# Batched 64x64 matmul: A loaded as row pairs, half-empty block stationaries, one store per group

## The chip, the cores and the metric

The kernel runs on one core of one Trainium2 chip. The metric is the device time of one execution in microseconds (us); smaller is better. A batch is one of 1024 independent products; a group is the 32 batches that one turn of the kernel's loop handles.

## The reference

Inputs `a` and `b` are float32 arrays of 1024 x 64 x 64, drawn from a normal distribution. The output is `np.matmul(a, b)` in float32: 1024 independent products C = A B of 64 x 64 matrices.

```
a = randn(1024, 64, 64); b = randn(1024, 64, 64)
return np.matmul(a, b).astype(np.float32)
```

The arithmetic on the chip is in bfloat16 with float32 sums: the loads convert float32 to bfloat16 on their way into SBUF.

## The kernel before

The loop over 32 groups is written out in full (Python `range`), so every instruction below stands 32 times in the program. Tiles come from pools that rotate: three buffers for the inputs (`a_in`, `b_in`), two for the transposed A in SBUF (`at_sb`), three for the output tile (`c_sb`), two for each of the two PSUM tiles (`at_psum`, `c_psum`). A planner derives all semaphores from which instruction reads and writes which tile; each engine works through its instructions in the order of the program, and POOL issues its DMAs in that order too.

One group does this:

- **Loads (L52, L60), issued from POOL.** Two DMAs bring `a`, two bring `b`, in the order a, b, a, b. Each fills 64 of the 128 partitions: partition = a row of a matrix, then 16 matrices, then the 64 elements of the row. One row of one matrix is contiguous in DRAM, so each DMA moves 1024 pieces of 64 float32, 256 bytes read and 128 bytes (bfloat16) written.
- **Transposes (L71) on TensorE.** A matrix multiply contracts over the partition, so A is needed with k on the partitions. Eight 128x128 transposes (against an identity) turn the 32 matrices of `a_in` into `at_psum`, one PSUM bank.
- **Copy (L77) on DVE.** One copy of 128 x 1024 bfloat16 brings `at_psum` into `at_sb`.
- **Products (L86) on TensorE.** 32 matmuls with a 64 x 64 stationary (A transposed) and a 64-column moving operand (B). Even and odd batches use opposite halves of the partitions and write opposite halves of `c_psum`.
- **Copy (L95) on ACT.** One copy of 128 x 1024 float32 brings `c_psum` (two banks) into `c_sb`.
- **Stores (L98), issued from SP.** Two DMAs, one for each half of the partitions, with 1024 pieces of 256 bytes each.

Ahead of the loop POOL builds the identity. On TensorE the transposes of a group stand in the program behind the matmuls of the group before.

Of the kernel before, what the change touches and what calls it, by code (L numbers as in the profile page):

```python
# [1 line left out]

# [5 lines left out]


@with_exitstack
def kernel(
    ctx: ExitStack,
    tc: tile.TileContext,
    a: bass.AP,
    b: bass.AP,
    out: bass.AP,
):
    nc = tc.nc

    B, M, K = a.shape
    _, _, N = b.shape
    assert (M, K, N) == (64, 64, 64)

    GROUP = 32
    HALF = GROUP // 2
    NT = HALF // 2
    dt_in = mybir.dt.bfloat16
    n_groups = B // GROUP

    BATCH_ELEMS = M * K

    consts = ctx.enter_context(tc.tile_pool(name="consts", bufs=1))
    ab_pool = ctx.enter_context(tc.tile_pool(name="ab", bufs=3))
    at_pool = ctx.enter_context(tc.tile_pool(name="at", bufs=2))
    c_pool = ctx.enter_context(tc.tile_pool(name="c", bufs=3))
    psum_t = ctx.enter_context(tc.tile_pool(name="psum_t", bufs=2, space=bass.MemoryType.PSUM))
    psum_c = ctx.enter_context(tc.tile_pool(name="psum_c", bufs=2, space=bass.MemoryType.PSUM))

    identity = consts.tile([128, 128], dt_in)  # L40
    make_identity(nc, identity)

    def dram_ap(tensor_ap: bass.AP, offset: int, dims):
        return bass.AP(tensor=tensor_ap.tensor, offset=offset, ap=[list(d) for d in dims])

    for g in range(n_groups):
        base = g * GROUP

        a_in = ab_pool.tile([128, HALF, 64], dt_in, name="a_in")
        b_in = ab_pool.tile([128, HALF, 64], dt_in, name="b_in")  # L50
        for h in (0, 1):
            nc.gpsimd.dma_start(  # L52
                out=a_in[64 * h : 64 * h + 64, :, :],
                in_=dram_ap(
                    a,
                    (base + HALF * h) * BATCH_ELEMS,
                    [[64, 64], [BATCH_ELEMS, HALF], [1, 64]],
                ),
            )
            nc.gpsimd.dma_start(  # L60
                out=b_in[64 * h : 64 * h + 64, :, :],
                in_=dram_ap(
                    b,
                    (base + h) * BATCH_ELEMS,
                    [[64, 64], [2 * BATCH_ELEMS, HALF], [1, 64]],
                ),
            )

        at_psum = psum_t.tile([128, NT, 128], dt_in, name="at_psum")
        for t in range(NT):  # L70
            nc.tensor.transpose(  # L71
                at_psum[:, t, :],
                a_in[:, 2 * t : 2 * t + 2, :],
                identity,
            )
        at_sb = at_pool.tile([128, NT, 128], dt_in, name="at_sb")
        nc.vector.tensor_copy(out=at_sb, in_=at_psum)  # L77

        c_psum = psum_c.tile([128, 2, 8, 64], mybir.dt.float32, name="c_psum")
        for i in range(GROUP):  # L80
            h = i % 2
            tblk = (i % HALF) // 2
            chalf = i // HALF
            bank = i // 16
            slot = (i // 2) % 8
            nc.tensor.matmul(  # L86
                out=c_psum[64 * h : 64 * h + 64, bank, slot, :],
                lhsT=at_sb[64 * h : 64 * h + 64, tblk, 64 * chalf : 64 * chalf + 64],
                rhs=b_in[64 * h : 64 * h + 64, i // 2, :],
                start=True,  # L90
                stop=True,
            )

        c_sb = c_pool.tile([128, 2, 8, 64], mybir.dt.float32, name="c_sb")
        nc.scalar.copy(out=c_sb, in_=c_psum)  # L95

        for h in (0, 1):
            nc.sync.dma_start(  # L98
                out=dram_ap(
                    out,  # L100
                    (base + h) * BATCH_ELEMS,
                    [[64, 64], [2 * BATCH_ELEMS, 16], [1, 64]],
                ),
                in_=c_sb[64 * h : 64 * h + 64, :, :, :],
            )


# [1 line left out]
_INS = ['a', 'b']  # L109
_OUTS = [((1024, 64, 64), 'float32')]  # L110


# [23 lines left out]
```

## Time and profile before

| what | value |
|---|---|
| device time, median of 4 runs | 222.24 us (221.8 to 222.96) |
| the profiled execution, device time | 222.3 us |
| the profiled execution, span of its instructions | 220.5 us |
| TensorE matmul busy | 31% of the span |
| DVE busy, ACT busy | 10%, 15% |
| POOL busy (issuing loads) | 47% |
| read from HBM, written to HBM | 33.55 MB, 16.78 MB |

The span runs from the first to the last instruction; the device time of the same execution is 1.8 us longer. Busy shares are averages over the whole span. The DMA share of a stretch is the mean number of packets that one of the 16 DMA engines had in hand, so it can exceed 1. The GB/s of the profile count bytes as written, and a load writes half of the bytes that it reads. A packet here is one contiguous piece; each DMA adds 16 packets of 4 bytes that raise its semaphore.

### The profile page before, as it was taken

To read this page: it belongs to the slowest core of one execution; us is meant where nothing else is said; L and a number is where in the kernel's file an instruction comes from. 1 tells how busy PE (TensorE), PEld (TensorE's weight loads), DVE (VectorE), ACT (ScalarE), POOL (GpSimd) and SP (SyncE) were. 2 spreads that over 40 slices of the span, in tenths; PEclk is the share of its full clock that TensorE was granted. 3 is DMA by queue.
4 is the path that set the end of the run, shared out by engine and by line. 5 is a ranking of instruction groups with operands and counts; after the bars stand their busy time and mean duration, and the time that the engine had idled before them with its cause. 6 is when DMAs were issued, how large, how long until landed. Compare 5 with 4: busy or idle time off the path is not lost.

```text
span 220.5 us, 3108 instructions
## 1 busy us (share of the span) xinstructions
PE 68.1 (31%) x1280; PEld 55.1 (25%) x1280; DVE 22.1 (10%) x32; ACT 33.7 (15%) x33; POOL 104.7 (47%) x134
## 2 busy tenths in 40 slices
PE   0462231233441134431234422233422233322340
PEld 0352121123331133321133322133312133311230
DVE  0120011011110111110111110111110111100110
ACT  2111110111101111101111101111011111011110
POOL 8997434365444455444455435454445554441000
DMA  8999999999999999999999999999999999999974
GB/s 53 146 184 157 157 158 158 157 159 156 158 158 157 158 157 159 156 157 157 159 156 157 159 157 158 157 159 157 157 157 159 157 157 158 157 157 159 162 129 95
DMA packets 199695, 33.77 MB, mean 153 GB/s; under 512 B 199680, under 2 KB 199680, under 8 KB 199680
## 3 DMA queue, kind: packets, MB, share of 16 engines
q0 software_dynamic: 133120, 16.79, 117.8%
q1 hardware_dynamic: 66560, 16.78, 55.7%
q8 instruction: 10, 0.16, 0.3%
q14 instruction: 5, 0.04, 0.0%
HBM read 33.55 MB, written 16.78 MB: 228 GB/s over the span
## 4 chain that ended last, share of the span: by engine, by line
DMA 88%; POOL 5%; issue 3%; PE 0%; ACT 0%; POOLq 0%; ACTq 0%
DMA a_in<-in_a_dram 78%; DMA b_in<-in_b_dram 10%; POOL a_in L52 3%; POOL b_in L60 2%; PE c_psum L86 0%; ACT c_sb L95 0%; POOL identity masks.py:199 0%; POOL identity masks.py:197 0%; POOLq masks.py:199 0%; ACTq L95 0%; POOLq L131 0%; POOLq L60 0%; POOLq L120 0%
## 5 line engine op out<-in xcount | busy, mean ns | idle before, releaser
L60 POOL DMA_DIRECT2D b_in<-in_b_dram x64 | 52.9, 827 | 52.3 <-DMA b_in<-in_b_dram 50.7
L52 POOL DMA_DIRECT2D a_in<-in_a_dram x64 | 53.0, 828 | 42.4 <-DMA a_in<-in_a_dram 37.6
L71 PE MATMUL at_psum<-identity,a_in 128*128 128x128 bf16 x256 | 32.4, 306 | 118.0 <-DMA a_in<-in_a_dram 118.0
L95 ACT COPY c_sb<-c_psum 128x1024 f32<-128x1024 f32 x32 | 32.4, 1012 | 180.6 <-PE c_psum L86 180.6
L71 PEld LDWEIGHTS <-a_in 128*128 128x128 bf16 x256 | 24.8, 137 | 121.3 <-issue 121.3
L86 PE MATMUL c_psum<-b_in,at_sb 64*64 64x64 bf16 x1024 | 35.8, 239 | 27.8 <-DVE at_sb L77 25.1
L77 DVE COPY at_sb<-at_psum 128x1024 bf16<-128x1024 bf16 x32 | 22.1, 691 | 190.1 <-PE at_psum L71 190.1
L86 PEld LDWEIGHTS <-at_sb 64*64 64x64 bf16 x1024 | 30.3, 151 | 37.5 <-DVE at_sb L77 33.6
L95 ACT ACT_TABLE_LOAD x1 | 1.3, 1283 | 0.7 <-PEq L120 0.7
masks.py:199 POOL TENSOR_SCALAR_AFFINE_SELECT identity<-identity 128x128 bf16<-128x128 bf16 x1 | 0.3, 306 | 0.1
masks.py:197 POOL MEMSET identity<- 128x128 bf16 x1 | 0.2, 205 | 0.3 <-POOLq L120 0.3
L120 POOL MEMSET const-float32-0.0<- 128x1 f32 x1 | 0.1, 99 | 0.2 <-issue 0.2
L120 POOL MEMSET const-bfloat16-1.0<- 128x1 bf16 x1 | 0.1, 102 | 0.0
L120 POOL MEMSET const-uint8-127<- 128x1 uint8 x1 | 0.1, 102 | 0.0
L120 POOL MEMSET const-float32-1.0<- 128x1 f32 x1 | 0.1, 99 | 0.0
## 6 DMA issues: line engine op xcount, KB each, us to landing
out_dram<-c_sb SPq DMA_DIRECT2D x64, 256.0 KB, 9.7
a_in<-in_a_dram POOLq DMA_DIRECT2D x64, 128.0 KB, 12.8
b_in<-in_b_dram POOLq DMA_DIRECT2D x64, 128.0 KB, 12.9
```

Of the source, the lines that this page charges most:

```text
L52: nc.gpsimd.dma_start(out=a_in[64 * h : 64 * h + 64, :, :], in_=dram_ap(a, (base + HALF * h) * BATCH_ELEMS, [[64, 64], [BATCH_ELEMS, HALF] ...
L60: nc.gpsimd.dma_start(out=b_in[64 * h : 64 * h + 64, :, :], in_=dram_ap(b, (base + h) * BATCH_ELEMS, [[64, 64], [2 * BATCH_ELEMS, HALF], [ ...
L71: nc.tensor.transpose(at_psum[:, t, :], a_in[:, 2 * t : 2 * t + 2, :], identity,)
L77: nc.vector.tensor_copy(out=at_sb, in_=at_psum)
L86: nc.tensor.matmul(out=c_psum[64 * h : 64 * h + 64, bank, slot, :], lhsT=at_sb[64 * h : 64 * h + 64, tblk, 64 * chalf : 64 * chalf + 64], ...
L95: nc.scalar.copy(out=c_sb, in_=c_psum)
L120: nc = _bacc.Bacc("TRN2", target_bir_lowering=False, num_devices=1)
```

## The change

- **Loads of A.** `a_pk` holds two consecutive rows of one matrix on each partition: partition p of block u has the 128 consecutive float32 that start at element 128 p of the four matrices 4u to 4u+3. Four DMAs per group, each for two blocks and all 128 partitions, replace two; each has 256 pieces of 512 bytes read and 256 bytes written. The order on POOL becomes a, a, b, a, a, b. The loads of B stay as they are.
- **Transposes.** Still eight of 128x128. Each now gives even rows of four matrices on partitions 0 to 63 and odd rows on 64 to 127.
- **Copies from PSUM.** One DVE copy becomes four copies of 64 partitions x 512 elements, two on DVE and two on ACT, into two tiles: `se_sb` for the even rows and `so_sb` for the odd rows. For each pair of batches the first one's k stands on partitions 0 to 63 with columns 0 to 31, the second one's on partitions 64 to 127 with columns 32 to 63. The other two quarters hold zeros.
- **Zeros.** The three pairs of these tiles are allocated once, and 12 memsets on DVE ahead of the loop write their zeros.
- **Products.** Still 32 matmuls with 64 columns each way, but each contracts over all 128 partitions: two batches at a time, even rows or odd rows. The output has 32 rows of each batch.
- **Copies of C.** One ACT copy becomes a DVE copy and an ACT copy, one for each bank of `c_ps`. They interleave even and odd rows in `c_sb`, so that each partition holds two consecutive rows.
- **Stores.** One DMA of 128 partitions per group replaces two; it has 1024 pieces of 512 bytes.

Buffer counts stay: three for inputs and output, two for each PSUM tile; the stationary tiles have three where `at_sb` had two.

```diff
-        a_in = ab_pool.tile([128, HALF, 64], dt_in, name="a_in")
+        a_pk = ab_pool.tile([128, NBLK, 128], dt_mm, name="a_pk")
+        AW = 2
         for h in (0, 1):
-            nc.gpsimd.dma_start(
-                out=a_in[64 * h : 64 * h + 64, :, :],
-                in_=dram_ap(
-                    a,
-                    (base + HALF * h) * BATCH_ELEMS,
-                    [[64, 64], [BATCH_ELEMS, HALF], [1, 64]],
-                ),
-            )
+            for u in range(h * NBLK // 2, (h + 1) * NBLK // 2, AW):
+                nc.gpsimd.dma_start(
+                    out=a_pk[:, u : u + AW, :],
+                    in_=dram_ap(
+                        a,
+                        (base + 4 * u) * BE,
+                        [[128, 128], [4 * BE, AW], [1, 128]],
+                    ),
+                )
...
+    for i in range(ST_BUFS):
...
+        nc.vector.memset(se_i[0:64, :, 32:64], 0.0)
+        nc.vector.memset(se_i[64:128, :, 0:32], 0.0)
+        nc.vector.memset(so_i[0:64, :, 32:64], 0.0)
+        nc.vector.memset(so_i[64:128, :, 0:32], 0.0)
...
-        nc.vector.tensor_copy(out=at_sb, in_=at_psum)
+        nc.vector.tensor_copy(out=st_dst(se_sb, 0, 0), in_=at_src(0, 0))
+        nc.scalar.copy(out=st_dst(se_sb, 64, 32), in_=at_src(0, 1))
+        nc.scalar.copy(out=st_dst(so_sb, 0, 0), in_=at_src(64, 0))
+        nc.vector.tensor_copy(out=st_dst(so_sb, 64, 32), in_=at_src(64, 1))
...
+        for s in range(NPAIR):
+            hc = s % 2
+            slot = s // 2
+            for eps, st_tile in ((0, se_sb), (1, so_sb)):
+                nc.tensor.matmul(
+                    out=c_ps[64 * hc : 64 * hc + 64, eps, slot, :],
+                    lhsT=st_tile[:, s, :],
+                    rhs=b_in[:, s, :],
...
-        nc.scalar.copy(out=c_sb, in_=c_psum)
+        nc.vector.tensor_copy(out=c_sb[:, :, 0, :], in_=c_ps[:, 0])
+        nc.scalar.copy(out=c_sb[:, :, 1, :], in_=c_ps[:, 1])
-        for h in (0, 1):
-            nc.sync.dma_start(
...
+        nc.sync.dma_start(
+            out=dram_ap(
+                out,
+                base * BE,
+                [[128, 128], [4 * BE, NPAIR // 2], [1, 128]],
+            ),
+            in_=c_sb,
+        )
```

## Rows read from the trace of the kernel before

**Rows 1.** The page: shares of the span in the chain that ended last.
```profile
DMA 88%; POOL 5%; issue 3%; PE 0%; ACT 0%; POOLq 0%; ACTq 0%
```
**Rows 2.** The page's DMA queues: packets, MB, share of 16 engines' span.
```profile
q0 software_dynamic: 133120, 16.79, 117.8%
q1 hardware_dynamic: 66560, 16.78, 55.7%
```
**Rows 3.** Stretches: busy of PE, PEld, DVE, ACT, POOL; granted clock, DMA share, GB/s.
```profile
11.00:13.00 2.00, 1.22 (x22) 0.95 (x22) 0.69 (x1) 0.00 (x0) 2.00 (x4) 1.00 2.43 155
...
40.00:60.00 20.00, 6.42 (x120) 5.18 (x120) 2.07 (x3) 3.60 (x4) 10.13 (x14) 1.00 1.89 157
100.00:120.00 20.00, 6.43 (x120) 5.18 (x120) 2.08 (x3) 2.96 (x4) 9.55 (x13) 1.00 1.84 157
180.00:200.00 20.00, 6.22 (x120) 5.10 (x120) 2.07 (x3) 2.93 (x4) 9.55 (x12) 1.00 1.80 158
...
216.50:218.50 2.00, 0.00 (x0) 0.00 (x0) 0.00 (x0) 0.00 (x0) 0.00 (x0) 1.00 0.95 203
```
**Rows 4.** DMA queue of code loading in the 1 us from 57.5: packets, MB, share.
```profile
q14 instruction: 1, 0.01, 1.9%
```
**Rows 5.** Chain that ended last, in order of time: start, us, what.
```profile
11.50 0.69 POOL a_in L52
12.19 7.55 DMA b_in<-in_b_dram
...
19.77 0.49 issue
20.26 0.80 POOL b_in L60
21.06 15.68 DMA a_in<-in_a_dram
36.74 0.28 issue
37.03 13.19 DMA a_in<-in_a_dram
```
**Rows 6.** Line L52: durations of its DMA instruction in ns; issue to landing in us.
```profile
L52 POOL DMA_DIRECT2D a_in<-in_a_dram x64: 808/811/990, 1.3 to 197.1; - x64
...
DMA to landing us min/median/max: 3.3/12.8/17.4
```
**Rows 7.** Timeline of one group in the middle: start, us, engine, line, what [idle before].
```profile
104.08 1.01 PE L71 MATMUL at_psum<-identity,a_in 128*128 128x128 bf16 x8 [4.60 <-DMA a_in<-in_a_dram]
...
105.13 0.69 DVE L77 COPY at_sb<-at_psum 128x1024 bf16<-128x1024 bf16 x1 [6.76 <-PE at_psum L71]
105.62 0.81 POOL L60 DMA_DIRECT2D b_in<-in_b_dram  x1 [0.57 <-DMA b_in<-in_b_dram]
105.88 0.93 PEld L86 LDWEIGHTS <-at_sb 64*64 64x64 bf16 x32 [1.05 <-DVE at_sb L77]
105.88 1.06 PE L86 MATMUL c_psum<-b_in,at_sb 64*64 64x64 bf16 x32 [0.78 <-DVE at_sb L77]
...
107.03 1.01 ACT L95 COPY c_sb<-c_psum 128x1024 f32<-128x1024 f32 x1 [6.44 <-PE c_psum L86]
```
**Rows 8.** Timeline of the opening.
```profile
0.24 0.10 POOL L120 MEMSET const-float32-0.0<- 128x1 f32 x1 [0.24 <-issue]
...
0.74 0.20 POOL masks.py:197 MEMSET identity<- 128x128 bf16 x1 [0.29 <-POOLq L120]
...
1.29 0.94 POOL L52 DMA_DIRECT2D a_in<-in_a_dram  x1 [0.34 <-issue]
...
8.06 0.69 DVE L77 COPY at_sb<-at_psum 128x1024 bf16<-128x1024 bf16 x1 [8.06 <-PE at_psum L71]
```
**Rows 9.** Timeline of the end.
```profile
212.93 1.01 PE L86 MATMUL c_psum<-b_in,at_sb 64*64 64x64 bf16 x31 [0.34 <-DMA b_in<-in_b_dram]
...
214.03 1.01 ACT L95 COPY c_sb<-c_psum 128x1024 f32<-128x1024 f32 x1 [6.17 <-PE c_psum L86]
```

More of the change, by code (lines that the diff above doesn't have):

```diff
@@ L8 @@
 from concourse._compat import with_exitstack
+GROUP = 32
+AB_BUFS = 3
+ST_BUFS = 3
+C_BUFS = 3
+PS_T_BUFS = 2
+PS_C_BUFS = 2
 @with_exitstack
@@ L23 @@
     assert (M, K, N) == (64, 64, 64)
[L25 to L28, printed above, removed]
+    NBLK = GROUP // 4
+    NPAIR = GROUP // 2
+    dt_mm = mybir.dt.bfloat16
     n_groups = B // GROUP
-    BATCH_ELEMS = M * K
+    BE = M * K
     consts = ctx.enter_context(tc.tile_pool(name="consts", bufs=1))
[L34 to L40, printed above, removed]
-    make_identity(nc, identity)
+    ab_pool = ctx.enter_context(tc.tile_pool(name="ab", bufs=AB_BUFS))
+    st_pool = ctx.enter_context(tc.tile_pool(name="st", bufs=ST_BUFS))
+    c_pool = ctx.enter_context(tc.tile_pool(name="c", bufs=C_BUFS))
+    psum_t = ctx.enter_context(tc.tile_pool(name="psum_t", bufs=PS_T_BUFS, space=bass.MemoryType.PSUM))
+    psum_c = ctx.enter_context(tc.tile_pool(name="psum_c", bufs=PS_C_BUFS, space=bass.MemoryType.PSUM))
+    identity = consts.tile([128, 128], dt_mm)
+    make_identity(nc, identity)
+    se_tiles = []
+    so_tiles = []
+    for i in range(ST_BUFS):
+        se_i = st_pool.tile([128, NPAIR, 64], dt_mm, name=f"se_sb{i}")
+        so_i = st_pool.tile([128, NPAIR, 64], dt_mm, name=f"so_sb{i}")
+        nc.vector.memset(se_i[0:64, :, 32:64], 0.0)
+        nc.vector.memset(se_i[64:128, :, 0:32], 0.0)
+        nc.vector.memset(so_i[0:64, :, 32:64], 0.0)
+        nc.vector.memset(so_i[64:128, :, 0:32], 0.0)
+        se_tiles.append(se_i)
+        so_tiles.append(so_i)
     def dram_ap(tensor_ap: bass.AP, offset: int, dims):
@@ L47 @@
         base = g * GROUP
-        a_in = ab_pool.tile([128, HALF, 64], dt_in, name="a_in")
-        b_in = ab_pool.tile([128, HALF, 64], dt_in, name="b_in")
+        a_pk = ab_pool.tile([128, NBLK, 128], dt_mm, name="a_pk")
+        b_in = ab_pool.tile([128, NPAIR, 64], dt_mm, name="b_in")
+        AW = 2
         for h in (0, 1):
-            nc.gpsimd.dma_start(
-                out=a_in[64 * h : 64 * h + 64, :, :],
-                in_=dram_ap(
-                    a,
-                    (base + HALF * h) * BATCH_ELEMS,
-                    [[64, 64], [BATCH_ELEMS, HALF], [1, 64]],
-                ),
-            )
+            for u in range(h * NBLK // 2, (h + 1) * NBLK // 2, AW):
[7 more added lines that the diff above has]
+                )
             nc.gpsimd.dma_start(
@@ L63 @@
                     b,
-                    (base + h) * BATCH_ELEMS,
-                    [[64, 64], [2 * BATCH_ELEMS, HALF], [1, 64]],
-                ),
-            )
[L69 to L74, printed above, removed]
-            )
-        at_sb = at_pool.tile([128, NT, 128], dt_in, name="at_sb")
-        nc.vector.tensor_copy(out=at_sb, in_=at_psum)
@@ L79 @@
[L79 to L91, printed above, removed]
-            )
@@ L94 @@
-        c_sb = c_pool.tile([128, 2, 8, 64], mybir.dt.float32, name="c_sb")
-        nc.scalar.copy(out=c_sb, in_=c_psum)
-        for h in (0, 1):
-            nc.sync.dma_start(
[L99 to L105, printed above, removed]
+                    (base + h) * BE,
+                    [[64, 64], [2 * BE, NPAIR], [1, 64]],
+                ),
+            )
@@ new lines, with at_src @@
+        at_ps = psum_t.tile([128, NBLK, 128], dt_mm, name="at_ps")
+        for u in range(NBLK):
+            nc.tensor.transpose(at_ps[:, u, :], a_pk[:, u, :], identity)
+        se_sb = se_tiles[g % ST_BUFS]
+        so_sb = so_tiles[g % ST_BUFS]
+        def at_src(part_lo, v_first):
+            t = at_ps[part_lo : part_lo + 64, :, :]
+            return bass.AP(
+                tensor=t.tensor,
+                offset=t.offset + v_first * 32,
+                ap=[t.ap[0], t.ap[1], [64, 2], [1, 32]],
+            )
@@ new lines, in st_dst @@
+        def st_dst(tile_, part_lo, col_lo):
+            t = tile_[part_lo : part_lo + 64, :, :]
+            return bass.AP(
+                tensor=t.tensor,
+                offset=t.offset + col_lo,
+                ap=[t.ap[0], [128, NBLK], [64, 2], [1, 32]],
+            )
+        nc.vector.tensor_copy(out=st_dst(se_sb, 0, 0), in_=at_src(0, 0))
+        nc.scalar.copy(out=st_dst(se_sb, 64, 32), in_=at_src(0, 1))
+        nc.scalar.copy(out=st_dst(so_sb, 0, 0), in_=at_src(64, 0))
+        nc.vector.tensor_copy(out=st_dst(so_sb, 64, 32), in_=at_src(64, 1))
@@ new lines @@
+        c_ps = psum_c.tile([128, 2, NPAIR // 2, 64], mybir.dt.float32, name="c_ps")
+        for s in range(NPAIR):
[6 more added lines that the diff above has]
+                    rhs=b_in[:, s, :],
+                    start=True,
+                    stop=True,
+                )
+        c_sb = c_pool.tile([128, NPAIR // 2, 2, 64], mybir.dt.float32, name="c_sb")
@@ L109 @@
+        nc.vector.tensor_copy(out=c_sb[:, :, 0, :], in_=c_ps[:, 0])
[7 more added lines that the diff above has]
+            in_=c_sb,
+        )
 _INS = ['a', 'b']
```

## The prediction

> **What bounds the kernel now.** I read the chain of waits first, because its shares say what the end hangs on: 88% of the span is waiting for DMAs, and PE and ACT have none of it [rows 1]. The second view is the stretches. From 40 to 200 us the rate stands at 157 to 158 GB/s whichever 20 us are taken, while PE is busy for under a third of the time and ACT for a sixth [rows 3]. A rate that flat, with every DMA engine holding about 1.8 packets, means that the 16 engines always have work and set the pace. The third view is the queues: 133120 load packets and 66560 store packets, 199680 in all, and none of them carries more than 256 bytes on the DRAM side [rows 2]. So the question is what a packet costs, and how that depends on its size.
>
> A group writes 33.55 MB / 32 = 1.049 MB by the profile's count (half of it bfloat16 into SBUF, half float32 into DRAM). At 157.5 GB/s that is 6.66 us, and 32 groups are 213.1 us. The span is 220.5 us, so opening and end together cost 7.4 us beside the steady work, and the device time adds 1.8 us. The profiled execution took 222.3 us and the median of the runs is 222.24, so a forecast against the profile is one against the median.
>
> **Prices of a packet.** From 11 to 13 us only loads run, at 155 GB/s [rows 3]: 155 / 16 engines / 128 bytes gives one load packet (256 bytes read) per 13.2 ns and engine. A group has 256 load and 128 store packets per engine (the 4-byte packets, 6 per engine before and 7 after, are inside these prices). Loads at that price take 256 x 13.2 = 3.38 us; what is left of 6.66 is 3.28 us for 128 stores, or 25.6 ns for a store of 256 bytes beside loads. Near the end stores run alone at 203 GB/s [rows 3], 20.2 ns each.
>
> No row has a data packet of 512 bytes. By count it would cost what 256 bytes cost; by bytes, twice that: 13.2 to 26.4 ns for a load, 20.2 to 51.2 ns for a store. The row that parts them is one code packet of 8192 bytes, which held its engine for 1.9% of 16 x 1 us = 0.30 us in the middle of the stream [rows 4]: 0.037 ns a byte, 9.5 ns for each further 256 bytes. On that slope 9.5 of a load's 13.2 ns go by bytes and 3.7 by packet, while a store has about 16 ns that do not go by bytes. I take it: 13.2 + 9.5 = 22.7 ns for a 512-byte load and 25.6 + 9.5 = 35.1 ns for a 512-byte store.
>
> **The change, part by part.**
>
> DMA work per group and engine, after. A: four DMAs of 256 pieces are 64 packets x 22.7 = 1.45 us (before 128 x 13.2 = 1.69). B is unchanged, 128 x 13.2 = 1.69 us. Stores: 64 x 35.1 = 2.25 us (before 3.28). Sum 5.39 us in place of 6.66; most of the gain is in the stores. The bounds: all by count with the store-only price, 64 x 13.2 + 1.69 + 64 x 20.2 = 3.8 us; all by bytes, 6.66 us.
>
> The row says that stores, not loads, carry a cost that bytes do not explain [rows 3, 4]. The Trainium skill, DMA: Bandwidth & Descriptors, section Specifications, puts line rate at 512 bytes and says that below it the engine does a read-modify-write. By that rule a 512-byte store would drop the extra altogether, which is the first rival below.
>
> POOL. A load instruction of 1024 pieces takes 0.81 us [rows 6]. Two of B stay, 1.62 us. The four of A have 256 pieces each: between 0.20 us (by pieces) and 0.81 us (all fixed), so POOL needs 2.4 to 4.9 us per group. Both lie under 5.39, so DMA hides them. If DMA fell to 4.6 us the upper end would set the pace at 4.9.
>
> The loads' queue. The chain shows each load waiting for the one eight issues before: the b issued at 12.19 lands at 19.77 and lets the b at 20.26 go, the a at 21.06 lands at 36.74 and lets the one at 37.03 go, and this repeats through the run [rows 5]. Eight DMAs were two groups; with six per group they are 1.33 groups, 7.2 us of DMA work at 5.39. A landing takes 3.3 us when the queue is empty [rows 6], plus 0.28 us to issue, so the engines still find work in the rings. I price the shorter queue at 0, at most 0.3 us a group where the large B loads bunch up.
>
> PE's own chain. The transposes of a group stand behind the matmuls of the group before, so transposes, copies and matmuls of one group follow each other on PE: before 1.01 + 0.69 + 1.06 us and gaps of about 0.05, 2.9 us in all [rows 7], hidden under 6.66. After: the transposes stay at 1.01. A copy of half the elements costs DVE 0.35 to 0.69 us and ACT 0.51 to 1.01 [rows 7]; with a start-up of 0.1 us, as one element on POOL takes [rows 8], that is 0.40 and 0.56. Side by side the four copies take 1.12 us, one after the other 1.92. The matmuls lie between 1.06 us as now and 32 x 1.01 / 8 = 4.04 at the spacing of the 128-column transposes; with half the columns I take half of that spacing, 2.0 us, because the two row halves no longer run as separate matmuls. With five gaps of 0.06 the chain is 4.4 to 5.2 us. It stays below 5.39, but barely: the cover that was 3.7 us thick is nearly gone.
>
> All four copies read the one bank that the transposes wrote, and before it had one reader. The Trainium skill, PSUM — Partial Sum Buffer, section Terms, forbids two engines in one bank at once on the same partitions; by that rule the planner would line up the copies that share partitions, which leads towards the 5.2 us end; no row of before shows it.
>
> DVE and ACT in sum. DVE gets two half copies and one of 128 x 512 float32 (at most 1.01, as ACT's 1024 elements), under 2.4 us; ACT three halves, under 3.1. Hidden.
>
> Opening and end. Twelve memsets at 0.20 (POOL's, nearest) to 0.69 us (a DVE copy, twice the size) are 2.4 to 8.3 us on DVE, which had nothing to do until 8.06 us [rows 8]; at the upper end they delay the first copy by about 1 us, I take 0. The first load is issued as before at 1.29. At the end, matmuls +0.9 us, the final copy -0.4, the last stores 64 x 29.7 in place of 128 x 20.2 ns, -0.7 [rows 3, 9]: together 0.
>
> Sum: 32 x 5.39 = 172.5, + 7.4 + 1.8 = 181.7, so I say **181 us**. Its own range is 172 to 192 (store between 32 and 38 ns, load between 21 and 25).
>
> **Rivals.**
>
> 1. The whole extra of a small store goes at 512 bytes. Then a store costs 22.7 (like a load of that size) to 25.6 ns, the DMA work is 4.6 to 4.8 us, and the time 156 to 162; PE's chain at 5.2 or POOL at 4.9 would stop it first, up to 176. For it: the 16 ns that bytes do not explain. Against: stores alone are cheaper already at 256 bytes (20.2), so part of the cost is the alternation of queues, which the size does not remove.
>
> 2. PE's chain is the bound on the faster side: lined-up copies near 0.6 and 0.8 us, or a matmul spacing above 63 ns, give 5.6 to 6.6 us and 188 to 220 us. For it: a cover of 0.2 to 1 us. Against: the copies have half the work, and the planner could move transposes ahead.
>
> 3. PE's chain makes it slower. Copies at full price and lined up are 2 x 0.69 + 2 x 1.01 = 3.4 us; with 4.04 us of matmuls and 1.01 of transposes the chain is 8.7 us, 32 x 8.7 + 9.2 = 288 us. It decides from 5.39 us on and is slower than now from 6.66. Against: both upper ends are needed at once, though the sizes halved.
>
> 4. The change does not do what it says for time: the engines are bound by bytes, 6.66 us a group, 222 us. For it: bytes are the same. Against: the 8 KB packet moved at 27 bytes per ns where loads reach 256 / 13.2 = 19.4 [rows 3, 4].
>
> **How the numbers follow.** The forecast has 0.50, rival 1 0.26, rival 2 0.16, rival 3 0.04, rival 4 0.04. The range 157 to 204 takes in the forecast, nearly all of rival 1 and half of rival 2. About 0.5% is what a measurement of this kernel can tell from no change. Faster by more than that: 0.50 + 0.26 + 0.16 = 0.92; within it: 0.04, rival 4; slower: 0.04, rival 3.
>
> **What would show it.** In the profile after: 131072 data packets, and 65536 of them of b; a rate near 1.049 MB / 5.39 us = 195 GB/s held through the middle, and DMA near 88% of the chain again. Under rival 1 the rate is 219 GB/s or more, or PE, DVE and ACT appear in the chain. Under rivals 2 and 3 the DMA share has gaps and PE's transposes no longer wait for a load. POOL's time for an A load tells how much of 0.81 us is fixed; the store's issue to landing tells its price. The forecast is wrong if the middle runs below 185 or above 205 GB/s, or if loads land in bursts because eight are too few.

## The result, and the profile after

The changed kernel takes 173.03 us (median of 11 runs, 171.4 to 174.2) against 222.15 (16 runs): a ratio of 0.776, 95% interval 0.774 to 0.779. The forecast was 181 us, range 157 to 204. The direction holds, and so do the packets' prices. But the middle of the run was faster than the prediction's own limit allows, and 8 us of the gain came from a place that the forecast had priced at nothing.

The page of the changed kernel: busy time of POOL, packets, queues, and the shares of the chain that ended last, which answer to [rows 1, 2]. The profiled execution took 171.88 us, its span is 170.0.

```profile
PE 83.0 (49%) x1280; PEld 51.9 (31%) x1280; DVE 52.4 (31%) x108; ACT 57.1 (34%) x97; POOL 143.8 (85%) x198
...
DMA packets 134671, 33.77 MB, mean 199 GB/s; under 512 B 101888, under 2 KB 134656, under 8 KB 134656
...
q0 software_dynamic: 101376, 16.79, 128.7%
q1 hardware_dynamic: 33280, 16.78, 35.5%
...
DMA 42%; POOL 41%; issue 13%; PE 1%; POOLq 1%; ACT 0%
```

Packets fell from 199680 to 134656 for the same bytes; without the 4-byte ones that is 131072, as the prediction counted. But the chain is no longer DMA alone. DMA has 42% and POOL 41%, and POOL is busy for 85% of the span.

The costliest groups of the changed kernel, by line: busy time, mean ns of one, idle time before. They answer to [rows 6, 7].

```profile
L71 POOL DMA_DIRECT2D a_pk<-in_a_dram x128 | 92.6, 738 | 12.2 <-DMA b_in<-in_b_dram 5.7
...
L79 POOL DMA_DIRECT2D b_in<-in_b_dram x64 | 55.3, 865 | 0.8 <-DMA a_pk<-in_a_dram 0.3
...
L114 DVE COPY so_sb<-at_ps 64x512 bf16<-64x512 bf16 x32 | 13.7, 428 | 42.9 <-ACT so_sb L113 42.9
L112 ACT COPY se_sb<-at_ps 64x512 bf16<-64x512 bf16 x32 | 18.5, 577 | 20.4 <-DVE se_sb L111 19.4
L111 DVE COPY se_sb<-at_ps 64x512 bf16<-64x512 bf16 x32 | 13.3, 417 | 20.5 <-PE at_ps L90 19.8
L113 ACT COPY so_sb<-at_ps 64x512 bf16<-64x512 bf16 x32 | 18.6, 582 | 0.8
```

A load of 256 pieces costs POOL 0.74 us where one of 1024 pieces costs 0.87 (0.81 before): nearly all of it is fixed. Six loads are 4 x 0.738 + 2 x 0.865 = 4.68 us per group; their ends overlap a little, and POOL's busy time is 143.8 / 32 = 4.5 us per group. The four copies cost what was estimated, and the releasers show them one after the other: DVE, ACT, ACT, DVE (L111 to L114).

The stretches of the changed kernel answer to [rows 3]: busy time of PE, PEld, DVE, ACT and POOL, granted clock, DMA share, GB/s.

```profile
40.00:60.00 20.00, 10.29 (x161) 6.55 (x160) 5.91 (x12) 6.98 (x12) 17.96 (x25) 1.00 1.80 215
100.00:120.00 20.00, 10.60 (x170) 6.72 (x172) 6.14 (x12) 6.98 (x12) 17.73 (x25) 1.00 1.75 219
150.00:151.00 1.00, 0.61 (x5) 0.18 (x4) 0.38 (x1) 0.55 (x1) 0.99 (x2) 1.00 1.39 301
152.00:154.00 2.00, 0.46 (x3) 0.26 (x3) 0.43 (x1) 1.05 (x2) 1.30 (x3) 1.00 2.07 170
```

At 215 GB/s a group takes 1.049 MB / 215 = 4.88 us, where the forecast had 5.39 and before had 6.66. The prediction called itself wrong if the middle ran above 205 GB/s, and it does. POOL is busy for 18 of every 20 us. And the rate is no longer flat: it swings between 170 and 301 GB/s inside 4 us. The queues of these two short stretches (packets, MB, share) show the mix, first 150 to 151 us, then 152 to 154:

```profile
q1 hardware_dynamic: 533, 0.27, 93.0%
q0 software_dynamic: 225, 0.03, 45.8%
```

```profile
q0 software_dynamic: 1860, 0.32, 202.0%
q1 hardware_dynamic: 46, 0.02, 4.7%
```

In the first, 533 of 758 packets are stores (q1); in the second, 46 of 1906. So loads and stores no longer keep a steady mix. The time from issue to landing points the same way: a load of B, which the change leaves as it was, lands after 5.6 us in the median instead of 12.9, so the load queue is shorter. The lines are before's, then two of the changed kernel:

```profile
b_in<-in_b_dram POOLq DMA_DIRECT2D x64, 128.0 KB, 12.9
...
out_dram<-c_sb SPq DMA_DIRECT2D x32, 512.0 KB, 5.9
...
b_in<-in_b_dram POOLq DMA_DIRECT2D x64, 128.0 KB, 5.6
```

### The profile page after: what moved, and what is told of

It reads as the page before. It is cut to its first block, busy times and chain, and to the rows that moved or that the text cites. A ratio compares the mean times of both kernels' runs of the same rounds, so it can differ in the third digit from the quotient of the medians.

```text
span 170.0 us, 3303 instructions
## 1 busy us (share of the span) xinstructions
PE 83.0 (49%) x1280; PEld 51.9 (31%) x1280; DVE 52.4 (31%) x108; ACT 57.1 (34%) x97; POOL 143.8 (85%) x198
## 2 busy tenths in 40 slices
DMA packets 134671, 33.77 MB, mean 199 GB/s; under 512 B 101888, under 2 KB 134656, under 8 KB 134656
## 3 DMA queue, kind: packets, MB, share of 16 engines
q1 hardware_dynamic: 33280, 16.78, 35.5%
HBM read 33.55 MB, written 16.78 MB: 296 GB/s over the span
## 4 chain that ended last, share of the span: by engine, by line
DMA 42%; POOL 41%; issue 13%; PE 1%; POOLq 1%; ACT 0%
DMA b_in<-in_b_dram 31%; POOL a_pk L71 25%; POOL b_in L79 16%; DMA a_pk<-in_a_dram 11%; PE at_ps L90 1%; POOLq L166 0%; ACT c_sb L131 0%; POOL identity masks.py:199 0%; POOL identity masks.py:197 0%; POOLq masks.py:199 0%; POOLq L79 0%; POOLq L155 0%
## 5 line engine op out<-in xcount | busy, mean ns | idle before, releaser
L71 POOL DMA_DIRECT2D a_pk<-in_a_dram x128 | 92.6, 738 | 12.2 <-DMA b_in<-in_b_dram 5.7
L121 PE MATMUL c_ps<-b_in,se_sb 128*64 128x64 bf16 x512 | 39.6, 242 | 56.0 <-DMA b_in<-in_b_dram 28.0
L90 PE MATMUL at_ps<-identity,a_pk 128*128 128x128 bf16 x256 | 45.4, 303 | 21.6 <-DMA a_pk<-in_a_dram 19.6
L121 PEld LDWEIGHTS <-se_sb 128*64 128x64 bf16 x512 | 31.9, 153 | 63.9 <-ACT so_sb L113 41.9
L131 ACT COPY c_sb<-c_ps 128x512 f32<-128x512 f32 x32 | 18.8, 586 | 86.8 <-issue 79.8
L130 DVE COPY c_sb<-c_ps 128x512 f32<-128x512 f32 x32 | 22.1, 692 | 47.6 <-PE c_ps L121 47.6
L121 PE MATMUL c_ps<-b_in,so_sb 128*64 128x64 bf16 x512 | 34.0, 242 | 3.9 <-DVE so_sb L114 3.9
L121 PEld LDWEIGHTS <-so_sb 128*64 128x64 bf16 x512 | 29.8, 155 | 10.5 <-DVE so_sb L114 7.2
L114 DVE COPY so_sb<-at_ps 64x512 bf16<-64x512 bf16 x32 | 13.7, 428 | 42.9 <-ACT so_sb L113 42.9
L112 ACT COPY se_sb<-at_ps 64x512 bf16<-64x512 bf16 x32 | 18.5, 577 | 20.4 <-DVE se_sb L111 19.4
L111 DVE COPY se_sb<-at_ps 64x512 bf16<-64x512 bf16 x32 | 13.3, 417 | 20.5 <-PE at_ps L90 19.8
L113 ACT COPY so_sb<-at_ps 64x512 bf16<-64x512 bf16 x32 | 18.6, 582 | 0.8
```

What stands on the lines that cost most here:

```text
L71: nc.gpsimd.dma_start(out=a_pk[:, u : u + AW, :], in_=dram_ap(a, (base + 4 * u) * BE, [[128, 128], [4 * BE, AW], [1, 128]],),)
L90: nc.tensor.transpose(at_ps[:, u, :], a_pk[:, u, :], identity)
L111: nc.vector.tensor_copy(out=st_dst(se_sb, 0, 0), in_=at_src(0, 0))
L112: nc.scalar.copy(out=st_dst(se_sb, 64, 32), in_=at_src(0, 1))
L113: nc.scalar.copy(out=st_dst(so_sb, 0, 0), in_=at_src(64, 0))
L114: nc.vector.tensor_copy(out=st_dst(so_sb, 64, 32), in_=at_src(64, 1))
```

## The experiments

The first theory after the result was **P**: POOL's issue sets the pace. Its rivals were **D** (the packets' prices are lower than forecast) and **C** (PE's chain). Four runs were made to part them.

**Two loads of A per group.**

```diff
-        AW = 2
+        AW = 4
```

> The changed kernel with two loads of A per group (four blocks, 512 pieces of 512 bytes each) in place of four; nothing else differs. Theory P (POOL's issue sets the pace of the changed kernel: 4 x 0.74 + 2 x 0.865 = 4.69 us of POOL per group where a group takes 4.88): POOL falls to about 2 x 0.76 + 1.73 = 3.25 us, the next bound is the DMA work or PE's chain near 4.4 to 4.6 us, and the time is 150 to 157 us. Theory D (the DMA engines' packets set the pace, as forecast, at 4.88 instead of 5.39 us): the packets are the same, 170 to 175 us. Theory C (PE's chain of transposes, copies and matmuls): unchanged too, 170 to 175 us.

Measured: 183.8 us (ratio to before 0.828, 0.826 to 0.831). All three theories missed: less work on POOL made it 11 us slower. POOL was relieved (56% busy) and the rate fell:

```profile
40.00:60.00 20.00, 8.52 (x143) 5.98 (x139) 5.62 (x11) 6.34 (x11) 10.90 (x15) 1.00 1.74 198
100.00:120.00 20.00, 9.43 (x159) 6.68 (x157) 5.67 (x11) 6.40 (x12) 12.02 (x16) 1.00 1.68 197
```

The columns are as above. 1.049 MB / 197.5 is 5.31 us per group, near the forecast's sum of 5.39. The loads wait longer to land, and so do the stores, which are the same DMAs as in the changed kernel:

```profile
out_dram<-c_sb SPq DMA_DIRECT2D x32, 512.0 KB, 8.4
...
b_in<-in_b_dram POOLq DMA_DIRECT2D x64, 128.0 KB, 9.7
```

**Eight loads of A per group.**

```diff
-        AW = 2
+        AW = 1
```

> The changed kernel with eight loads of A per group (one block, 128 pieces of 512 bytes each) in place of four: the suspected cost is doubled, the bytes and data packets stay. Theory P with a load instruction that is nearly all fixed cost: POOL needs 8 x 0.70 + 1.73 = 7.3 us per group, the time is about 32 x 7.3 + 9 = 243 us, slower than the kernel before the change. Theory D: 172 to 176 us. Theory C: 172 to 176 us.

Measured: 213.5 us. P's direction is right; P's size was off because a load of 128 pieces costs 0.61 us, not 0.70. The lines of POOL in this run:

```profile
L71 POOL DMA_DIRECT2D a_pk<-in_a_dram x256 | 141.9, 612 | 8.0 <-issue 5.1 <-DMA b_in<-in_b_dram 1.6 <-DMA a_pk<-in_a_dram 0.9
L79 POOL DMA_DIRECT2D b_in<-in_b_dram x64 | 58.5, 914 | 2.2 <-issue 1.2 <-DMA a_pk<-in_a_dram 1.0
```

8 x 0.612 + 2 x 0.914 is 6.72 us, and 32 of them are 215 us; without the overlap of their ends POOL is busy for 190.7 of 213.3 us. So POOL does bind at ten loads per group; at six it is near. This run does not refute D for six loads, because here POOL's need rose above the DMA work too. C is answered by the changed kernel's own trace: its products wait 28.0 us in all for loads of B and its transposes 19.6 us for loads of A, so PE's chain is not what paces it.

**One load of A and one of B per group.**

```diff
-        for h in (0, 1):
...
+        nc.gpsimd.dma_start(
+            out=a_pk[:, :, :],
+            in_=dram_ap(a, base * BE, [[128, 128], [4 * BE, NBLK], [1, 128]]),
+        )
+        nc.gpsimd.dma_start(
+            out=b_in[:, :, :],
+            in_=dram_ap(b, base * BE, [[64, 128], [2 * BE, NPAIR], [1, 64]]),
+        )
```

> The changed kernel with one load of A (1024 pieces of 512 bytes) and one of B (128 partitions, 2048 pieces of 256 bytes) per group, two load instructions in place of six. Theory P: POOL needs at most 2 us per group and is out of the way; the time is set by DMA or by PE's chain, within 3 us of the run with two loads of A, 148 to 157 us, or up to 4 us above it because transposes wait for a whole load of A. Theories D and C: 170 to 175 us.

Measured: 182.6 us (0.821 to 0.829). Every theory missed again, and now POOL is out of the way for certain. The trace showed what the first one had not: with two loads per group the queue of loads is deep, and there are stretches in which as many loads as stores pass. From 96 to 98 us of this run, rate and queues:

```profile
96.00:98.00 2.00, 0.00 (x0) 0.00 (x0) 0.00 (x0) 1.14 (x2) 0.89 (x2) 0.50 1.39 213
```

```profile
q1 hardware_dynamic: 557, 0.29, 69.4%
q0 software_dynamic: 558, 0.14, 69.3%
```

558 loads of A against 557 stores: one for one. 32 us of engine time / 557 is 57.5 ns for a pair, and the forecast's prices give 22.7 + 35.1 = 57.8. From this came theory **X**: the 35.1 ns of a store hold while packets of two queues take turns, and a kernel whose load queue runs empty from time to time lets the stores run alone, more cheaply.

**The copies left out.**

```diff
+        if g < ST_BUFS:
+            nc.vector.tensor_copy(out=st_dst(se_sb, 0, 0), in_=at_src(0, 0))
...
```

> The kernel with two loads of A per group, and the four copies from the transposes' bank are left out after the third group, so the products of later groups use stationaries of the first three: a part of the computation is missing, all transfers and the other instructions stay. PE's chain per group loses about 2.1 us. If PE's chain is the bound once POOL is relieved, the time falls by 5 us or more below the run with two loads of A. If the DMA work is the bound then, it stays within 2 us of it. Under theory P for the changed kernel either may hold; under theory C for the changed kernel the time falls to 150 us or less here while the run with two loads of A stays at 172.

Measured: 184.8 us, 1 us from the run with two loads of A. PE's chain does not bind there. (From the fourth group on, the output of this kernel is not the product.)

**The prices alone.** A kernel of transfers only: 32 loads each of

```diff
+            in_=dram_ap(b, g * GROUP * BE, [[64, 128], [2 * BE, NPAIR], [1, 64]]),
...
+            in_=dram_ap(a, g * GROUP * BE, [[128, 128], [4 * BE, NBLK], [1, 128]]),
```

and then stores of 16 groups in pieces of 64 floats and of 16 groups in pieces of 128.

> Transfers alone, one kind after the other; no product is computed and the output is not the reference's. First all of B in pieces of 256 bytes (converting loads, 2048 pieces per DMA), then all of A in pieces of 512 bytes, then stores of half the output in pieces of 256 bytes, then of the other half in pieces of 512 bytes. It measures the terms of the forecast's sum with no other queue beside them. By the forecast: load of 256 bytes 13.2 ns per engine (155 GB/s as written), load of 512 bytes 22.7 ns (180 GB/s), store of 256 bytes alone 20.2 ns (203 GB/s), store of 512 bytes alone 29.7 ns (276 GB/s). Theory X (a store beside loads costs more because the engine changes between the two queues packet by packet, and a changed kernel whose loads run short escapes it): the same four numbers. Theory R (a store under 512 bytes costs extra of itself, and at 512 bytes it does not): the 512-byte store alone costs no more than the 256-byte one, 20 ns (400 GB/s).

The four stretches, one per kind, in that order (busy time of DVE and POOL, clock, DMA share, GB/s):

```profile
20.00:50.00 30.00, 0.00 (x0) 20.86 (x20) 1.00 2.45 156
60.00:95.00 35.00, 0.00 (x0) 21.07 (x25) 1.00 1.82 181
115.00:140.00 25.00, 0.00 (x0) 0.00 (x0) 1.00 0.97 216
150.00:175.00 25.00, 0.00 (x0) 0.00 (x0) 1.00 1.00 282
```

Per engine: 128 x 16 / 156 = 13.1 ns for a load of 256 bytes, 256 x 16 / 181 = 22.6 for one of 512 (forecast 22.7), 256 x 16 / 216 = 19.0 for a store of 256, 512 x 16 / 282 = 29.0 for one of 512 (forecast 29.7). Theory R falls: alone, the larger store costs 10 ns more. So the slope of 9.5 ns per 256 bytes, read from one code packet [rows 4], came out for both directions (9.5 for loads, 10.0 for stores). That it did is partly luck: it was one packet, and the engines held 1.89 packets each on the average in that part of the run [rows 3], so the time for which it was held need not be what it cost.

**The store's part alone.** A in pieces of 256 bytes again:

```diff
+            nc.gpsimd.dma_start(
+                out=a_pk[:, :, 64 * h : 64 * h + 64],
+                in_=dram_ap(
+                    a,
+                    base * BE + 64 * h,
+                    [[128, 128], [4 * BE, NBLK], [1, 64]],
+                ),
+            )
```

> The changed kernel with A loaded in pieces of 256 bytes as before (two DMAs of 1024 pieces per group, even rows and odd rows; order a, b, a, b), stores still in pieces of 512 bytes: the store's part of the change alone. Forecast's sum with the load queue full: 256 x 13.2 + 64 x 35.1 = 5.63 us per group, 32 x 5.63 + 9.2 = 189 us. Theory X: 186 to 192 us, with stretches in which stores and loads take turns. Theory R: 256 x 13.2 + 64 x 25.6 = 5.02 us, 170 us.

Measured: 191.3 us. X and the sum hold (189), R does not (170).

**One queue.** Loads as in the run with one A and one B, the store issued from POOL behind the loads of the group two later, with four output buffers:

```diff
+    LAG = 2
...
+    def store(g):
+        nc.gpsimd.dma_start(
...
+        if g >= LAG:
+            store(g - LAG)
```

> The kernel with one load of A and one of B per group, and the store issued from POOL too, behind the loads, two groups late (four output buffers): the same packets, but loads and stores stand in one queue, so an engine has nothing to alternate between. Theory X: a 512-byte store costs its price alone, 27 to 30 ns in place of 35, a group 1.45 + 1.69 + 64 x 27 to 30 = 4.9 to 5.05 us, the time 163 to 171 us, clearly below the same kernel with stores on SP (182.6). Theory M (reads and writes cost more beside each other whatever queue they come from): 180 to 190 us. Theory Q (the changed kernel was faster than its two-load variants for their landing pattern, not for the queues): no gain here, 180 us or more.

Measured: 166.9 us (0.748 to 0.756), inside X's interval and outside those of M and Q. But it does not part them, because "the same packets" was not true. The page of this run has 103951 packets:

```profile
DMA packets 103951, 33.77 MB, mean 205 GB/s; under 512 B 99840, under 2 KB 99840, under 8 KB 103936
```

103936 - 99840 = 4096 packets carry the 16.78 MB of the stores, 4096 bytes each. POOL's store puts eight 512-byte pieces into a packet where SP's has one, so the gain can come from the queue or from the packets.

**Work added on POOL.** Two loads of A per group, and ahead of each load of B a memset of 128 x 768 elements that nothing reads:

```diff
+            nc.gpsimd.memset(idle, 0.0)
             nc.gpsimd.dma_start(
                 out=b_in[64 * h : 64 * h + 64, :, :],
```

> The kernel with two loads of A per group (183.8 us) and an extra memset of 128 x 768 elements on POOL ahead of each load of B, about 0.4 to 0.7 us each: work is added, nothing else changes. POOL then needs about 3.25 + 0.8 to 1.4 = 4.1 to 4.7 us per group, close to the 4.7 of the changed kernel. Theory X: the load queue runs short as in the changed kernel, stores run by themselves for longer, and the time falls to 170 to 180 us although work was added. Every other theory: no change or slower, 183 us or more.

Measured: 185.3 us, outside X's interval of 170 to 180. The memset took 0.81 us, so POOL needed 5.0 us per group by the durations added up, against the 4.7 that were to be copied; by POOL's busy time it was 147.3 us in all against 143.8, nearly the same. From 20 to 60 us the run kept the changed kernel's rate (214 and 213 GB/s), later it did not:

```profile
20.00:40.00 20.00, 9.85 (x161) 7.19 (x161) 6.14 (x12) 7.31 (x13) 20.00 (x27) 1.00 1.79 214
100.00:120.00 20.00, 9.23 (x160) 6.79 (x160) 5.94 (x12) 5.82 (x10) 16.60 (x22) 1.00 1.64 190
```

In the second row POOL itself stands idle for 3.4 of 20 us and the DMA share is lower. Loads of B landed 9.7 us after their issue in the median, as without the memset, so the load queue did not become short as in the changed kernel. X is thus neither confirmed nor refuted by this run, and no other run makes the queue short by itself.

**One queue, padded output tile.**

```diff
-        c_sb = c_pool.tile([128, NPAIR // 2, 2, 64], mybir.dt.float32, name="c_sb")
+        c_sb = c_pool.tile([128, NPAIR // 2, 136], mybir.dt.float32, name="c_sb")
```

> In the run with one queue the stores' packets were 4096 bytes (one partition's eight pieces) where SP's were 512, so two things had changed. Here the output tile is padded (136 in place of 128 floats per block), so that the pieces of a partition don't adjoin in SBUF and the store's packets are 512 bytes again; the queue is still POOL's alone. Theory X (taking turns between two queues is the cost): stores stay near their price alone, 29 ns, a group 1.45 + 1.69 + 64 x 27 to 29 = 4.9 to 5.0 us, 164 to 171 us. Theory P4 (the gain came from the larger packets): 178 to 186 us, as with stores on SP.

Measured: 167.8 us (0.748 to 0.758). It parts nothing: the page still counts 103951 packets with 4096 of 4096 bytes, so the padding did not split them.

**The load's part alone.** Two loads of A per group, stores in two DMAs of 256-byte pieces:

```diff
+        for eps in (0, 1):
+            nc.sync.dma_start(
+                out=dram_ap(
+                    out,
+                    base * BE + 64 * eps,
+                    [[128, 128], [4 * BE, NPAIR // 2], [1, 64]],
+                ),
+                in_=c_sb[:, eps],
+            )
```

> The kernel with two loads of A per group (pieces of 512 bytes), and the store in pieces of 256 bytes again (two DMAs of 1024 pieces, even rows and odd rows): the load's part of the change alone. Forecast's sum with the load queue full: 64 x 22.7 + 128 x 13.2 + 128 x 25.6 = 6.42 us per group, 32 x 6.42 + 9.2 = 215 us. With the other half alone (A in 256, stores in 512) at 191.3 and both at 183.8 this says whether the two parts add up: 222 - 191 = 31 us for the stores, 7 to 8 us for A.

Measured: 213.1 us. Larger stores alone gave 222.1 - 191.3 = 31 us, larger loads of A alone 9 us, both with a full load queue 38 to 41 us (183.8 to 181.1): they add up.

**One queue, deeper.**

```diff
-AB_BUFS = 3
-C_BUFS = 4
+AB_BUFS = 5
+C_BUFS = 5
...
-    LAG = 2
+    LAG = 3
```

> The run with one queue (166.9 us), where POOL waited 65 us for output tiles, with the store three groups behind its loads in place of two, five input buffers in place of three and five output buffers in place of four. If the engines idled for that wait, the group falls to the packets' sum, 1.45 + 1.69 + 1.5 to 1.6 = 4.65 to 4.75 us, and the time is 157 to 162 us. If PE's chain (1.0 + 2.1 + 1.06 us and gaps) is the bound by now, it stays at 164 to 168 us.

Measured: 155.0 us (ratio 0.696, 0.694 to 0.698), below the expected 157 to 162 and the fastest of all. The stretches of this run:

```profile
40.00:60.00 20.00, 10.82 (x189) 8.50 (x183) 7.25 (x14) 7.90 (x14) 12.62 (x14) 1.00 1.83 234
100.00:120.00 20.00, 10.87 (x194) 8.48 (x195) 6.70 (x14) 7.56 (x13) 13.73 (x15) 1.00 1.83 239
```

1.049 MB / 236.5 is 4.43 us per group. PE's chain is what paces this kernel now. The transposes of three successive groups start 4.42 and 4.40 us apart, and none of the three waits for a load:

```profile
102.24 1.04 PE L95 MATMUL at_ps<-identity,a_pk 128*128 128x128 bf16 x8
106.66 1.03 PE L95 MATMUL at_ps<-identity,a_pk 128*128 128x128 bf16 x8
111.06 1.03 PE L95 MATMUL at_ps<-identity,a_pk 128*128 128x128 bf16 x8
```

In the whole run the transposes wait for a load 8 times, 12.1 us in all, 5.6 of them in the opening. So the second case of the expectation had the right next bound, with a time put too high. The packets' price has only an upper bound here: less the loads (64 x 22.6 + 128 x 13.1 = 3.12 us), 1.31 us are left for 64 pieces, at most 20.4 ns per 512 bytes if the loads keep their price alone, less than SP's 29.0 alone.

**The same with the store on SP.** One word:

```diff
     def store(g):
-        nc.gpsimd.dma_start(
+        nc.sync.dma_start(
```

> The fastest kernel so far (155.0 us: one load of A and one of B per group, five input and five output buffers, store three groups late) with one word changed: the store is issued from SP again, so its packets are of 512 bytes in a queue of their own. Depth, order and buffers stay. Theory X (packets of two queues take turns, and a 512-byte store then costs 35.1 ns): the forecast's sum with a full load queue, 32 x 5.39 + 9.2 = 182 us, 178 to 185. If the gain of the fastest kernel came from its deeper buffers and not from the queue: 155 to 165 us.

Measured: 181.1 us (0.813 to 0.821), X's value to 1 us; the depth alone gives nothing. Moving the store to POOL, its queue and its larger packets together, is worth 26 us here, and could be worth more in a kernel that PE's chain does not stop.

## Why the prediction was right, and where it was off

- **Packets are priced by count and bytes: right. That DMA alone sets the pace: right only in part.** The prices alone came out at 13.1, 22.6 and 29.0 ns against 13.2, 22.7 and 29.7, and a pair of alternating packets at 57.5 against 57.8. Wherever the load queue is full, the sum 32 x 5.39 + 9.2 holds: 181.1, 182.6 and 183.8 us in three kernels with two or four loads per group, and within 2.3 us in the two kernels with half of the change. In the changed kernel itself POOL has 41% of the chain beside DMA's 42%, where the prediction expected DMA near 88%. Which of the two sets 4.88 us is not shown.
- **"I price the shorter queue at 0, at most 0.3 us a group": the step that failed.** It took the eight loads in flight to be enough, and looked for a loss only. With six issues of almost fixed cost POOL needs nearly the whole of a group's time, the load queue runs short, and the middle gains: 5.39 - 4.88 = 0.51 us per group, or 16 us. The store is the term of the sum that moved: if the engines never idled and the loads kept their price, a store cost (4.88 - 1.45 - 1.69) / 64 = 27 ns on the average in place of 35.1.
- **Why stores are cheaper there is open.** That kernels with fewer loads, longer queues and the same packets take some 10 us more is shown. That stores "run alone" is not enough as a reason: 29.0 ns alone would give 1.45 + 1.69 + 1.86 = 5.0 us, more than the 4.88 measured. From 150 to 151 us, 533 stores and 225 loads passed; at 29.0 and 13.1 ns they would need 18.4 us of engine time, and 16 engines have 16 us in that stretch. So some loads pass beside a stream of stores almost for nothing. Alone, SP's stores keep only one packet in hand per engine (0.97 and 1.00, loads 2.45 and 1.82), which would leave room for that; no run tests it.
- **Opening and end "together 0": too low.** They cost 170.0 - 32 x 4.88 = 13.8 us instead of 7.4 and take 6 of the 16 us back. Part of it is POOL in the opening: in the first 12.75 us it is busy for 11.8 with four loads of A per group as with two, but the rate is 83 GB/s with four and 106 with two. That 173 us lies inside the forecast's own range of 172 to 192 is therefore partly luck, two errors of opposite sign.
- **POOL's issue: bounded from 2.4 to 4.9 us, measured 4.68 by durations and 4.5 by busy time.** The rows before had only one size of DMA, so the fixed part could not be read, and the upper end was nearly true. The first rival's "POOL at 4.9 would stop it first" names the right engine, and its "up to 176" takes in the measured time.
- **PE's chain: copies right, matmuls too dear.** 0.42 and 0.58 us against 0.40 and 0.56, and lined up. The Trainium skill, PSUM — Partial Sum Buffer, section Terms, says that no two engines may access one bank in the same partitions at once, and gave the reason to expect that. The trace agrees as to the order: DVE waits 42.9 us in all for ACT's copy out of the same half of the bank. But that copy also writes the same tile, `so_sb`, and no run parts the two reasons. The matmuls were put at 2.0 us and take 1.2, hardly more than before. So the chain is 4.4 us, the lower end of its 4.4 to 5.2, as the run with deeper buffers shows. The first and the last of a group's 32 in the timeline of the changed kernel (start, us):

```profile
10.20 0.26 PE L121 MATMUL c_ps<-b_in,se_sb 128*64 128x64 bf16 x1
...
11.15 0.24 PE L121 MATMUL c_ps<-b_in,so_sb 128*64 128x64 bf16 x1
```

- **Rival 1 falls as a mechanism.** The Trainium skill, DMA: Bandwidth & Descriptors, section Specifications, puts line rate at 512 bytes and a read-modify-write below. Here a store alone goes from 19.0 to 29.0 ns, and beside loads from 25.6 to about 35: a rise as a load's, and nothing of the extra falls away at 512 bytes. By its number alone the changed kernel would look like rival 1 (27 ns a store against its 22.7 to 25.6, and 215 to 219 GB/s against its 219 or more); it takes the kernels with the same stores and fewer loads to tell.
- **Memsets, DVE and ACT in sum:** hidden as said; the 12 memsets took 0.27 us each.

Left open beside that: POOL's store differs from SP's in two things, its queue and its 4096-byte packets. The 26 us between the two last runs belong to both, and the padded tile did not separate them.

## What to carry to other kernels

Price a DMA packet as a fixed part plus bytes, from any two sizes that the trace holds, and ask of each price beside which queue it was taken. Loads and stores that pass one for one from two full queues cost more here than the two kinds alone; putting both on one queue, with deep buffers and the store some groups late, was worth more here than the larger pieces of A, though its larger packets may have a part in that. And where a DMA's issue costs 0.61 us for 128 pieces and 0.87 for 1024, count issues on the issuing engine before splitting a transfer. When one bound is relieved, look in the trace for the next: in the fastest kernel here it was PE's chain.

## What the runs showed of the hardware

- Taking 42 us of issue work off POOL (143.8 to 102.2 us busy) made the kernel 11 us slower; its load queue was fuller (9.7 us from issue to landing of a B load instead of 5.6).
- With two full queues the engines pass one packet of each for one of the other (557 against 558 packets in 2 us) at 57.5 ns a pair, where the two kinds alone cost 22.6 + 29.0 = 51.6. With few loads in the mix it is the other way: 533 stores and 225 loads passed in 1 us, 301 GB/s, where stores alone reach 282.
- A store from POOL moves eight 512-byte pieces as one packet, at most 20.4 ns per piece in the mean if loads keep their price alone, against 29.0 for SP's single pieces.
- In the run with one load of A and one of B the granted clock of TensorE was 1.00 (2.4 GHz) from 18 to 20 us and 0.50 (1.2 GHz) from 22 to 28 us; before it fell, PE had stood for 3.06 us, until 20.9 us, waiting for a load of A. The later run with the same loads had such waits of up to 6.3 us at a granted clock of 1.0 throughout, so these runs do not show what lowers it. The two profiled executions took 180.5 us at a mean clock of 0.57 and 179.9 at 1.0.
